# Retention stage of a float32 encoder block: three v groups moved to its front, its steps spaced two pieces apart, PSUM in two alternating pools

## The chip, the cores and the metric

The kernel runs on one core of one Trainium2 chip. The core has five engines with queues of their own: TensorE (PE: matmuls), VectorE (DVE), ScalarE (ACT), GpSimd (POOL) and SyncE (SP, here only for loads). The metric is the device time of one execution in microseconds; a version's time is the median of several executions.

## The reference

One layer of an encoder on x of 512 tokens by 2048 channels, float32:

```python
h = rmsnorm(x, norm_gain)
q, k, v, g_ret, c_b, c_c, c_x, g_conv, merge_logits = split(h @ w_in)   # 8 of 1024 columns, then 2 x 2048
o = bidirectional_retention(rotary(q), rotary(k) * 128**-0.5, v)        # 8 heads of 128, decay per head and direction
branch_ret = rmsnorm_per_head(o) * ret_gn_gain * silu(g_ret)
branch_conv = c_b * conv3(c_c * c_x) * silu(g_conv)                     # depthwise, along the tokens
merged = sum over n of sigmoid(merge_logits[n]) * (branches[n] @ w_branch[n])   # w_branch: 2 of 1024 x 2048
out = rmsnorm(x + merged @ w_out, final_gain)
```

## The kernel before, in words

**Arithmetic.** Each float32 product is made of three products of rounded parts (`mm3`, L165 to L167): high by high, high by low, low by high. Tensors that are multiplied exist as a high part, made by ACT (`split_to`, L160), and a low part, the rest, made by DVE (L161).

**Pieces.** All weights pass through one list, `pieces`: 512 KB each (4 tiles of 128 rows by 256 columns). SP loads a piece to `raw` (L125), ACT makes `whi`, DVE makes `wlo`, PE uses it. `run` works the list off: it loads up to three pieces ahead, splits two ahead, issues a piece's matmuls, and then the functions of one entry of the list `background`. A scheduler then orders the instructions of each engine by their readiness, so the engine's order isn't exactly that of the text.

**Stages.** (1) Stage A, to some 150 us: x is normalised to `h1`, `h00`, `h10` (parts of h transposed, in SBUF), and 4 k groups (`group`) and 2 v groups (`group_tok`) of w_in's columns are computed, 4 pieces each. The k groups go through `rotary_post`, the v groups through `v_post` (ACT, L481, four evictions from PSUM, scaled), to DRAM (`k_d`, `v_d`). In the background `token_forms` adds the token sums that the next stage wants (L293 to L301, then a split to `fm`), one for each of eight j. (2) The Strassen stage, to 954 us: 40 groups (`group_s`) for the remaining columns of w_in, 7 products instead of 8, 4 pieces each, 42 matmuls of 256 columns a piece, with sums of weights on DVE (L154 to L156) and `combine` (L280 to L287) on ACT and DVE after each group. The results are scaled and stored by POOL's queue (`gate_d`, `conv_d`, `g_d`, `q_d`). (3) The retention stage, to 1164 us: the groups of `w_branch[1]` (conv branch, `up_group(1, i)`, 2 pieces each of 24 matmuls of 512 columns) in turn with v groups 2 and 3 (4 pieces each of 48 matmuls of 256 columns), and in the background `retention_program`, the 8 heads. (4) The groups of `w_branch[0]` (retention branch), to 1251 us. (5) `w_out` and the final norm.

**One head** is made of: `fetch_head` (k and q from DRAM to `st`), `split_head` (to `kh`, `kl`, `qh`, `ql`), `decay_table` (`tb`), four `score` (three matmuls to `sp`, DVE multiplies with the table at L514, then a split to `sh`, `sl`), four `outp` (three matmuls `op <- sh, vh`), `square`, `rms_o` (two matmuls with `ones`, L542 and L543), and `finish`. 26 matmuls of 512 columns each head. DMA issues of POOL (`nc.gpsimd.dma_start`) go through one queue in order: loads of k, q, v, gates, the conv operand and stores of results.

**Order before the change.** `retention_program` deals 27 steps to 21 places in order:

```python
        n = 21
        return [[]] + [sum(steps[k * len(steps) // n : (k + 1) * len(steps) // n], []) for k in range(n)]
```

PSUM: a Strassen group takes two tiles of two banks each from a pool `p4` of four, in turn. That pool is closed and a pool of two, `psR`, and the retention's pool `rps` are opened at the retention stage.

Of the kernel before, what the change touches and what calls it, by code (L numbers as in the profile page):

```python
# [30 lines left out]
def hybrid_block_kernel(  # L31
# [43 lines left out]
    gate_d = dr.tile([2, KT, P, S], F32, name="gate_d")  # L75
    ret_d = dr.tile([GG, P, S], F32, name="ret_d")
    conv_d = dr.tile([GG, P, S], F32, name="conv_d")
# [91 lines left out]
    background = []  # L169
    later = []  # L170

# [5 lines left out]
    def run(upto):  # L177
        while state["used"] < upto:
            i = state["used"]
            while state["loaded"] < min(i + 4, state["limit"]):  # L180
                load(pieces[state["loaded"]])
                state["loaded"] += 1
            split_upto(i + (3 if i >= XC - 1 else 1))
            pieces[i]["use"](pieces[i])
            state["used"] += 1
            for x in later:
                x[0] -= 1
            while later and later[0][0] < 0:
                later.pop(0)[1]()
            if background:  # L190
                for f in background.pop(0):
                    f()
# [33 lines left out]
    def group_s(src, post):  # L226


        st = {}

        order = [
            (0, 0, "b11", "d4"), (0, 1, "b12", "a11"), (1, 1, "b22", "a12"), (1, 0, "u", "a22"),
            (3, 0, "z", "a7"), (3, 1, "w", "d6"), (2, 0, "v", "a1"),
        ]
        seen = [next(i for i, o in enumerate(order) if o[0] == b) for b in range(4)]
        for q in range(KT // 4):
            def use(pc, q=q):
                if q == 0:
                    tiles = [fin["p4"].tile([P, 2, S], F32, name="acc", tag="acc") for _ in range(2)]
                    st["acc"] = tiles if state["banks"] else tiles[::-1]  # L240
                    state["banks"] += 1
                for n, (bank, half, b, a) in enumerate(order):
                    acc = st["acc"][bank // 2][:, bank % 2, half * 256 : half * 256 + 256]
                    for r in range(2):
                        x = token_form(a, q + 4 * r)
                        mm3(
                            acc,
                            [weight_form(w, b, r) for w in pc["w"]],
                            (x[:, 0], x[:, 1]),
                            q == 0 and r == 0 and n in seen,  # L250
                            q == KT // 4 - 1 and r == 1,
                            skip_group_check=True,
                        )
# [252 lines left out]
    def score(h, m):  # L506
# [7 lines left out]
        nc.vector.scalar_tensor_tensor(s, sp, SCALE, hd["tb"][:, o0 : o0 + S], op0=ALU.mult, op1=ALU.mult)  # L514
        sh = rps["sb"].tile([P, S], F32R, name="sh", bufs=3)
        sl = rps["sb"].tile([P, S], F32R, name="sl", bufs=3)
        split_to(sh, sl, s)
# [9 lines left out]
    def square(h):  # L527
        hd = heads[h]
        sq = tmp()
        nc.scalar.activation(sq, hd["o"], AF.Square)  # L530
        sh = rps["sb"].tile([P, S], F32R, name="sh", bufs=3)
        sl = rps["sb"].tile([P, S], F32R, name="sl", bufs=3)
        nc.vector.tensor_copy(sh, sq)
        nc.vector.tensor_tensor(sl, sq, sh.bitcast(F32), op=ALU.subtract)
        hd["sq"] = (sh, sl)
# [15 lines left out]
    def finish(h):  # L551
# [7 lines left out]
        nc.vector.tensor_tensor(y, y, hd["g"], op=ALU.mult)  # L559
        if h < 4:  # L560
            nc.gpsimd.dma_start(out=ret_d[h], in_=y)
# [24 lines left out]
    def split_head(h):  # L586
        hd = heads[h]
        for n in ("k", "q"):
            hi = rps["sb"].tile([P, S], F32R, name=n + "h")
            lo = rps["sb"].tile([P, S], F32R, name=n + "l")  # L590
            split_to(hi, lo, hd[n + "f"])
            hd[n] = (hi, lo)
# [5 lines left out]
    def open_branch():  # L598
        br0 = rps["br0"] = big.tile([P, 2, GG, S], F32R, name="br0", tag="h1")
        brs[0] = lambda kt: [(0, br0[:, :, kt, :])]  # L600
        for i in range(2):
            load_branch(0, i)

    def retention_program():

        L = lambda f, *v: (lambda: f(*v))
        steps = [[] for _ in range(6 * (H // 2) + 3)]
        for i in range(H // 2):
            a, b = 2 * i, 2 * i + 1
            own = [  # L610
                [L(split_v, i), L(split_head, a), L(decay_table, a), L(fetch_head, b)],
                [L(score, a, 0), L(score, a, 1)],
                [L(outp, a, 0), L(outp, a, 1), L(score, a, 2), L(score, a, 3), L(fetch_g, a)],
                [L(outp, a, 2), L(outp, a, 3), L(square, a), L(split_head, b), L(decay_table, b)],
                [L(score, b, 0), L(score, b, 1), L(rms_o, a)] + ([L(fetch, i + 1), L(fetch_head, a + 2)] if b + 1 < H else []),
                [L(outp, b, 0), L(outp, b, 1), L(score, b, 2), L(score, b, 3), L(finish, a), L(fetch_g, b)],
                [L(outp, b, 2), L(outp, b, 3), L(square, b)],
                [L(rms_o, b)],
                [L(finish, b)],
            ]  # L620
            for k, s in enumerate(own):
                steps[6 * i + k] += s
        steps[16].insert(0, open_branch)
        n = 21
        return [[]] + [sum(steps[k * len(steps) // n : (k + 1) * len(steps) // n], []) for k in range(n)]

# [5 lines left out]
    for i in range(4):  # L632
# [4 lines left out]
        else:  # L637
            group(cols(BW, i), KT, hTf, kp)
    for i in range(2):
        group_tok(cols(2 * BW, i), v_post(i))  # L640
    n_a = len(pieces)
# [107 lines left out]

    for n in range(2):  # L750
        up_group(1, n, conv_up_post(n))
    for i in range(2, 4):
        group_tok(cols(2 * BW, i), v_post(i))
        up_group(1, i, conv_up_post(i))
    for i in range(4, 8):
        up_group(1, i, conv_up_post(i))
# [4 lines left out]

    def load_branch(n, i):
        d = (ret_d, conv_d)[n]
        t = T()
        nc.gpsimd.dma_start(out=t, in_=pair(d, i))
        k = slice(2 * i, 2 * i + 2)
# [103 lines left out]
    state["loaded"] = 1  # L870
    ps_x = tc.tile_pool(name="xps", bufs=4, space=PSUM)
    xps = ps_x.__enter__()
# [29 lines left out]
    log_decays()  # L902
    ps_x.__exit__(None, None, None)
    xst.close()
    for z in range(2):
# [8 lines left out]
    part["forms"] = fm[::-1]  # L914
    for j in range(KT // 2):
        background.extend([[lambda j=j: token_forms(j)], []])
    run(n_a)
    while background:
        for f in background.pop(0):
            f()  # L920
    psx.close()
    h10x.close()
    with tc.tile_pool(name="p4", bufs=4, space=PSUM) as p4:
        fin["p4"] = p4
        lr = ctx.enter_context(tc.tile_pool(name="lr", bufs=1, reuse_waits="tile"))
        fin["lr"] = lr
        fin["sd"] = lr.tile([P, 2 * WF], F32, name="sd", tag="ev")
        run(n_s)
    fms.close()
    hx.close()  # L930

    pools["ps"] = ctx.enter_context(tc.tile_pool(name="psR", bufs=2, space=PSUM))
    pools["wp"] = ctx.enter_context(tc.tile_pool(name="wpR", bufs=3, reuse_waits="tile"))
# [7 lines left out]
    for _ in range(3):  # L941
        load(pieces[state["loaded"]])
        state["loaded"] += 1
    for i in range(4):
        load_branch(1, i)
    split_upto(n_s + 2)
    while later:
        later.pop(0)[1]()
    rsx.close()
    ha = lr.tile([P, 2, 7, 256], F32R, name="h10", tag="ev")  # L950
    hb = lr.tile([P, WF], F32R, name="h10b", tag="raw4")
    hb = hb[:, :512].rearrange("p (z j s) -> p z j s", z=2, j=1)
    hold["h10"] = lambda j: hb[:, :, 0] if j == 7 else ha[:, :, j]
    for z in range(2):
        nc.gpsimd.dma_start(out=ha[:, z], in_=a21_d[z, 0:7].rearrange("j p s -> p j s"))
        nc.gpsimd.dma_start(out=hb[:, z], in_=a21_d[z, 7:8].rearrange("j p s -> p j s"))
    ret = ExitStack()
    rps["sb"] = ret.enter_context(tc.tile_pool(name="ret", bufs=2, side="right", reuse_waits="tile"))
    rps["p"] = ret.enter_context(tc.tile_pool(name="rps", bufs=2, space=PSUM))
    dist = rps["dist"] = rps["sb"].tile([P, TW], F32, name="dist", bufs=1)  # L960
# [4 lines left out]
    nc.gpsimd.iota(dist, pattern=[[1, TW]], base=-OFF, channel_multiplier=-1, allow_small_or_imprecise_dtypes=True)  # L965
    fetch(0)
    fetch_head(0)
    background.extend(retention_program())
    run(n_r - 2)
    while background:  # L970
        for f in background.pop(0):
            f()
    rps["stg"] = big.tile([P, 2, 2, 2, S], F32, name="stg", tag="h00")
    for i in range(2):
        load_merge(i)
    run(n_r)
    ret.close()
    bbx.close()
# [61 lines left out]
```

## Time and profile before

| what | us |
|---|---|
| median of 3 runs | 1435.68 |
| lowest and highest | 1434.04, 1437.82 |
| the profiled execution | 1437.88 |
| its span in the profile | 1436.1 |
| PE busy | 1401.9 |
| DVE busy | 1083.8 |
| ACT busy | 586.8 |
| POOL busy | 104.7 |

The profile is of one execution of its own; its span runs from the first to the last recorded instruction. "Busy" of PE is the time covered by its matmuls' records, which are pipelined: one starts before the record of the one before it has ended. PEclk, in windows, is the clock granted to PE as a share of its full 2.4 GHz. L12 is line 12 of the kernel before.

### The profile page before, as it was taken

How to read it: one execution, taken by the hardware profiler on the slowest of the kernel's cores; microseconds unless marked ns; L12 is line 12 of the kernel's file. 1: busy time of each engine (PE TensorE's matmuls, PEld its weight loads, DVE VectorE, ACT ScalarE, POOL GpSimd, SP SyncE). 2: the span in 40 equal slices, each digit the busy share in tenths (PEclk: the TensorE clock that was granted, in tenths of full speed). 3: DMA queues.
4: the chain of work that ended last, by engine and by line, in shares of the span. 5: the costliest groups of instructions: out<-in, count | busy, mean ns of one | idle time of the engine just before them, and what ended most of it. 6: DMA issues, size and time to landing. Idle time of an engine off the chain costs nothing.

```text
span 1436.1 us, 23571 instructions
## 1 busy us (share of the span) xinstructions
PE 1401.9 (98%) x9938; PEld 1315.1 (92%) x9938; DVE 1083.8 (75%) x1417; ACT 586.8 (41%) x590; POOL 104.7 (7%) x141
## 2 busy tenths in 40 slices
PE   8999999999999999999999999988998999999997
PEld 7899999999999999999999999977896788888886
DVE  4877789999899888898898998956786845523533
ACT  7343344444434334343343443444565532222421
POOL 0000000000000000000000000021113101111110
PEclk9999999999999999999999999999999999999999
DMA  7533433344334344333343333476437445553412
GB/s 246 166 118 120 131 118 118 118 122 143 118 118 133 106 142 135 118 118 118 122 141 120 118 118 119 135 231 213 138 128 241 146 148 191 186 215 98 155 66 102
DMA packets 151310, 202.36 MB, mean 141 GB/s; under 512 B 6900, under 2 KB 127780, under 8 KB 150564
## 3 DMA queue, kind: packets, MB, share of 16 engines
q1 hardware_dynamic: 132788, 143.17, 31.7%
q0 software_dynamic: 18384, 57.68, 11.7%
q8 instruction: 77, 1.26, 0.4%
q14 instruction: 29, 0.24, 0.1%
q10 hardware_dynamic: 32, 0.01, 0.0%
HBM read 170.43 MB, written 30.41 MB: 140 GB/s over the span
## 4 chain that ended last, share of the span: by engine, by line
PE 88%; DMA 4%; DVE 3%; issue 2%; ACT 1%; SPq 0%; POOL 0%; DVEq 0%; POOLq 0%; ACTq 0%
PE acc L165 29%; PE acc L167 29%; PE acc L166 29%; DMA raw<-in_w_in_dram 1%; DVE wlo L161 1%; DMA st<-k_d 1%; DMA v_d<-T 0%; DMA T<-conv_d 0%; DMA xb<-in_x_dram 0%; PE op L165 0%; DMA stg<-m_d 0%; PE op L166 0%; PE op L167 0%; PE xtp L384 0%; SPq L373 0%
## 5 line engine op out<-in xcount | busy, mean ns | idle before, releaser
L160 ACT ACTIVATE whi<-raw 128x1792 fp32r<-128x1792 f32 (+2 forms) x257 | 374.8, 1459 | 579.2 <-PE acc L166 425.5
L161 DVE TENSOR_TENSOR wlo<-raw,whi 128x1792 fp32r<-128x1792 f32 (+2 forms) x257 | 442.7, 1724 | 209.0 <-PE acc L167 83.6
L165 PE MATMUL acc<-fm,whi 128*128 128x256 f32 x1280 | 362.6, 283 | 1.7 <-ACT T L481 1.7
L167 PE MATMUL acc<-fm,wlo 128*128 128x256 f32 x1280 | 363.1, 284 | 0.4 <-DVE wlo L161 0.4
L166 PE MATMUL acc<-fm,whi 128*128 128x256 f32 x1280 | 362.1, 283 | 0.0
L165 PE MATMUL acc<-h,whi 128*128 128x256 f32 (+1 forms) x1152 | 330.0, 286 | 0.0
L167 PE MATMUL acc<-h,wlo 128*128 128x256 f32 (+1 forms) x1152 | 328.4, 285 | 0.0
L166 PE MATMUL acc<-h,whi 128*128 128x256 f32 (+1 forms) x1152 | 328.3, 285 | 0.0
L165 PEld LDWEIGHTS acc<-fm,whi 128*128 128x128 f32 x1280 | 245.2, 192 | 1.9 <-ACT T L481 1.9
L167 PEld LDWEIGHTS acc<-fm,wlo 128*128 128x128 f32 x1280 | 244.4, 191 | 0.6 <-DVE wlo L161 0.6
L166 PEld LDWEIGHTS acc<-fm,whi 128*128 128x128 f32 x1280 | 244.4, 191 | 0.0
L165 PEld LDWEIGHTS acc<-h,whi 128*128 128x128 f32 x1152 | 216.9, 188 | 2.5
L166 PEld LDWEIGHTS acc<-h,whi 128*128 128x128 f32 x1152 | 216.5, 188 | 2.6
L167 PEld LDWEIGHTS acc<-h,wlo 128*128 128x128 f32 x1152 | 216.4, 188 | 2.5
L154 DVE TENSOR_TENSOR raw<-raw 128x512 f32<-128x512 f32 x160 | 109.7, 686 | 18.7 <-DMA raw<-in_w_in_dram 18.4
L166 PE MATMUL acc<-wlo,mT 128*128 128x512 f32 (+1 forms) x272 | 103.5, 380 | 0.0
L165 PE MATMUL acc<-whi,mT 128*128 128x512 f32 (+1 forms) x272 | 103.0, 379 | 0.0
L167 PE MATMUL acc<-whi,mT 128*128 128x512 f32 (+1 forms) x272 | 102.1, 375 | 0.0
L167 PE MATMUL acc<-whi,h 128*128 128x256 f32 x252 | 71.0, 282 | 0.0
L166 PE MATMUL acc<-wlo,h 128*128 128x256 f32 x252 | 71.0, 282 | 0.0
L165 PE MATMUL acc<-whi,h 128*128 128x256 f32 x252 | 71.0, 282 | 0.0
L156 DVE TENSOR_TENSOR raw<-raw 128x256 f32<-128x256 f32 x160 | 67.8, 424 | 3.8
(205 smaller groups left out, 1763.6 us busy)
## 6 DMA issues: line engine op xcount, KB each, us to landing
raw<-in_w_in_dram SPq DMA_DIRECT2D x191, 512.0 KB, 3.8
raw<-in_w_branch_dram SPq DMA_DIRECT2D x32, 512.0 KB, 3.8
raw<-in_w_out_dram SPq DMA_DIRECT2D x32, 512.0 KB, 3.7
gate_d<-T POOLq DMA_DIRECT2D x16, 512.0 KB, 4.7
T<-gate_d POOLq DMA_DIRECT2D x8, 512.0 KB, 5.3
m_d<-T POOLq DMA_DIRECT2D x8, 512.0 KB, 3.7
stg<-gate_d POOLq DMA_DIRECT2D x8, 512.0 KB, 4.5
stg<-m_d POOLq DMA_DIRECT2D x8, 512.0 KB, 4.0
```

What stands on the lines that cost most here:

```text
L154: nc.vector.tensor_tensor(s[:, 0:2].rearrange("p f r x -> p r f x"), diag, both21, op=ALU.add)
L156: nc.vector.tensor_tensor(s[:, 2], b21, b12, op=ALU.add)
L160: pin(nc.scalar.activation(hi, src, AF.Copy))
L161: pin(nc.vector.tensor_tensor(lo, src, hi.bitcast(F32), op=ALU.subtract))
L165: pin(nc.tensor.matmul(acc, lh, rh, start=start, stop=False, **kw))
L166: pin(nc.tensor.matmul(acc, lh, rl, start=False, stop=False, **kw))
L167: pin(nc.tensor.matmul(acc, ll, rh, start=False, stop=stop, **kw))
```

## The change

- **Order of the pieces.** Stage A computes one v group, not two. The retention stage begins with three v groups (12 pieces), and the eight conv groups (16 pieces) follow.
- **Spacing of the steps.** `retention_program` has 29 steps, three per head, the first of which runs ahead of the stage's pieces, and the others one behind each of 28 pieces. A head's `score` stand in its steps 1 and 2, its `outp` in 3 and 4, `rms_o` in 6, `finish` in 7. `sh` and `sl` have 5 buffers instead of 3, the splits of k and q one instead of two. Within a step the functions are sorted by a rank.
- **Branch operands.** The four loads of the conv branch stand behind the pieces of the v groups, in places 0, 2, 4 and 6, their splits a place later; before, they stood ahead of the stage. Of the retention branch only heads 0 and 1 go through DRAM, not 0 to 3.
- **The queue at the stage's start.** Loads of head 0's k and q and of v are written ahead of the reload of `h10`.
- **PSUM.** `xps`, the pool of stage A's transposes, stands on the right side; behind it `px`, two tiles of two banks. Strassen groups take both tiles from `px` and from `psA` in turn. The retention stage's groups use `px`.
- **Token forms** are made in the order 0, 4, 1, 5, 2, 6, 3, 7.

```diff
-                    tiles = [fin["p4"].tile([P, 2, S], F32, name="acc", tag="acc") for _ in range(2)]
-                    st["acc"] = tiles if state["banks"] else tiles[::-1]
+                    pool = (fin["px"], pools["ps"])[state["banks"] % 2]
+                    st["acc"] = [pool.tile([P, 2, S], F32, name="acc", tag="acc") for _ in range(2)]
...
-        sh = rps["sb"].tile([P, S], F32R, name="sh", bufs=3)
-        sl = rps["sb"].tile([P, S], F32R, name="sl", bufs=3)
+        sh = rps["sb"].tile([P, S], F32R, name="sh", bufs=5)
+        sl = rps["sb"].tile([P, S], F32R, name="sl", bufs=5)
...
-        if h < 4:
+        if h < 2:
             nc.gpsimd.dma_start(out=ret_d[h], in_=y)
...
     def retention_program():
...
+        first = (outp, score, rms_o, square, fetch_branch, fetch, fetch_head, fetch_g, split_head, decay_table)
...
+        steps = [[] for _ in range(3 * H + 5)]
+        for h in range(H):
+            i = h // 2
             own = [
...
+                [L(split_head, h), L(decay_table, h)] + ([L(fetch_head, h + 1)] if h + 1 < H else []),
+                [L(score, h, 0), L(score, h, 1)],
+                [L(score, h, 2), L(score, h, 3), L(fetch_g, h)],
+                [L(outp, h, 0), L(outp, h, 1)],
+                [L(outp, h, 2), L(outp, h, 3), L(square, h)],
+                [],
+                [L(rms_o, h)],
+                [L(finish, h)],
             ]
+            if h % 2 == 0:
+                own[1].insert(0, L(split_v, i))
+            elif h + 1 < H:
+                own[1].append(L(fetch, i + 1))
             for k, s in enumerate(own):
-                steps[6 * i + k] += s
...
+                steps[3 * h + k] += s
...
-    for i in range(2):
-        group_tok(cols(2 * BW, i), v_post(i))
+    group_tok(cols(2 * BW, 0), v_post(0))
...
-    for n in range(2):
-        up_group(1, n, conv_up_post(n))
-    for i in range(2, 4):
+    for i in range(1, 4):
         group_tok(cols(2 * BW, i), v_post(i))
-        up_group(1, i, conv_up_post(i))
-    for i in range(4, 8):
+    for i in range(8):
         up_group(1, i, conv_up_post(i))
...
-    for j in range(KT // 2):
+    for j in (0, 4, 1, 5, 2, 6, 3, 7):
...
-    for i in range(4):
-        load_branch(1, i)
     split_upto(n_s + 2)
...
+    fetch_head(0)
+    fetch(0)
...
+    steps = retention_program()
+    for f in steps.pop(0):
+        f()
+    for i in range(4):
+        steps[2 * i].append(lambda i=i: fetch_branch(1, i))
+        steps[2 * i + 1].append(lambda i=i: split_branch(1, i))
+    background.extend(steps)
```

**How the instructions move.** POOL's queue at the start of the retention stage, before (`h10` and `h10b` are the two parts of the reload of `h10` from `a21_d`, `T<-conv_d` the loads of the conv operand, `st` those of k and q):

```order
L956 DMA h10b_10355<-a21_d_83 128x256 x2
L652 DMA gate_d_75<-T_10100 128x2x512
L765 DMA T_10329<-conv_d_77 128x2x512
L765 DMA T_10333<-conv_d_77 128x2x512
L955 DMA h10_10354<-a21_d_83 128x7x256
L652 DMA gate_d_75<-T_10295 128x2x512
...
L955 DMA h10_10354<-a21_d_83 128x7x256
...
L568 DMA T_10372<-v_d_82 128x1024
L584 DMA st_10374<-k_d_79 128x512
L584 DMA st_10376<-q_d_80 128x512
```

Two loads of the conv operand stand ahead of the reload's second part, v, k and q behind it. POOL's queue at the same place in the changed kernel:

```order
L953 DMA h10b_10124<-a21_d_83 128x256 x2
L650 DMA gate_d_75<-T_9876 128x2x512
L563 DMA T_10121<-v_d_82 128x1024
L759 DMA T_10230<-conv_d_77 128x2x512
L952 DMA h10_10123<-a21_d_83 128x7x256
L650 DMA gate_d_75<-T_10071 128x2x512
L579 DMA st_10117<-k_d_79 128x512
L579 DMA st_10119<-q_d_80 128x512
L952 DMA h10_10123<-a21_d_83 128x7x256
```

One load of the conv operand is left there, v has moved ahead of the reload, k and q stand between the reload's two parts.

PE in the retention stage before, from the first `sp` of a head in the middle of the stage to its first `op` (`b0` and `b1` are tiles of the conv operand, the matmuls into `acc` those of a conv piece):

```order
L165 MATMUL sp_10934<-qh_10854,kh_10850 128x512
L166 MATMUL sp_10934<-ql_10855,kh_10850 128x512
L167 MATMUL sp_10934<-qh_10854,kl_10851 128x512
L165 MATMUL acc_10996<-b0_10319,whi_10782 128x512
L166 MATMUL acc_10996<-b0_10319,whi_10782 128x512
...
L165 MATMUL sp_10944<-qh_10854,kh_10850 128x512
...
L165 MATMUL sp_10968<-qh_10854,kh_10850 128x512
...
L165 MATMUL sp_10978<-qh_10854,kh_10850 128x512
L165 MATMUL op_10961<-sh_10940,vh_10846 128x512
```

Matmuls of a conv piece stand singly between the scores, and the first `op` comes right behind the last `sp`'s first matmul. In the changed kernel the same for a head beside two v pieces (matmuls into `acc` from `h00`, `h1`):

```order
L165 MATMUL sp_10711<-qh_10641,kh_10637 128x512
L166 MATMUL sp_10711<-ql_10642,kh_10637 128x512
L167 MATMUL sp_10711<-qh_10641,kl_10638 128x512
L165 MATMUL sp_10721<-qh_10641,kh_10637 128x512
...
L165 MATMUL acc_10491<-whi_10566,h00_93 128x256
L166 MATMUL acc_10491<-wlo_10567,h00_93 128x256
...
L165 MATMUL sp_10810<-qh_10641,kh_10637 128x512
...
L165 MATMUL acc_10840<-whi_10653,h1_92 128x256
L166 MATMUL acc_10840<-wlo_10654,h1_92 128x256
...
L167 MATMUL acc_10840<-whi_10653,h1_92 128x256
L165 MATMUL op_10889<-sh_10717,vh_10744 128x512
L166 MATMUL op_10889<-sl_10718,vh_10744 128x512
```

Before, the first `op` stood among the scores of its own head; now two times 48 matmuls of v pieces lie between a score and the `op` that reads it.

DVE where stage A goes over into the Strassen stage, before (L293 to L301 the additions of a token form, L154 to L156 the weight sums of a Strassen piece, `fm` and `wlo` low parts):

```order
L301 TENSOR_TENSOR T_1432<-T_1428,T_1432 128x256
L154 TENSOR_TENSOR raw_1493<-raw_1493 128x2x2x128
L161 TENSOR_TENSOR fm_622<-T_1432,fm_622 128x1024
L161 TENSOR_TENSOR wlo_1441<-raw_1368,whi_1440 128x1024
L155 TENSOR_TENSOR raw_1493<-raw_1493 128x2x128
L156 TENSOR_TENSOR raw_1493<-raw_1493 128x256
L154 TENSOR_TENSOR raw_1547<-raw_1547 128x2x2x128
L161 TENSOR_TENSOR wlo_1496<-raw_1438,whi_1495 128x1024
...
L161 TENSOR_TENSOR wlo_1550<-raw_1493,whi_1549 128x1792
...
L161 TENSOR_TENSOR wlo_1607<-raw_1547,whi_1606 128x1792
```

The token form's split is through ahead of the first low part of a Strassen piece that stands here. In the changed kernel, where these lines have the numbers L288 to L296:

```order
L154 TENSOR_TENSOR raw_1317<-raw_1317 128x2x2x128
L154 TENSOR_TENSOR raw_1374<-raw_1374 128x2x2x128
...
L161 TENSOR_TENSOR wlo_1320<-raw_1253,whi_1319 128x1792
L161 TENSOR_TENSOR fm_625<-T_1311,fm_625 128x1024
...
L154 TENSOR_TENSOR raw_1452<-raw_1452 128x2x2x128
L161 TENSOR_TENSOR wlo_1377<-raw_1317,whi_1376 128x1792
L288 TENSOR_TENSOR T_1437<-h00_93 128x256
L288 TENSOR_TENSOR T_1437<-h10_113 128x256
L288 TENSOR_TENSOR T_1437<-h1_92 128x512
...
L294 TENSOR_TENSOR T_1441<-T_1437 128x512
...
L295 TENSOR_TENSOR T_1441<-T_1437,T_1441 128x256
L161 TENSOR_TENSOR wlo_1455<-raw_1374,whi_1454 128x1792
```

Before, the last token form was through ahead of the first Strassen piece's low part; now the last one's additions stand between the low parts of the second and the third piece.

## Rows read from the trace of the kernel before

**Rows 1.** The page, part 1: busy us (share of the span) xinstructions of each engine.

```profile
PE 1401.9 (98%) x9938; PEld 1315.1 (92%) x9938; DVE 1083.8 (75%) x1417; ACT 586.8 (41%) x590; POOL 104.7 (7%) x141
```

**Rows 2.** PE's waits: what waited and for what: us in total, times, longest us.

```profile
PE op L165 <- ACT sh L160: 9.9, 6, 2.6
...
PE acc L165 <- ACT T L481: 1.7, 1, 1.7
PE acc L165 <- DVE T L287: 1.6, 1, 1.6
```

**Rows 3.** Windows of the retention stage: from:to, us, each engine's busy us, PEclk, DMA share.

```profile
954.00:967.00 13.00, 7.56 (x31) 5.20 (x30) 6.80 (x8) 3.60 (x4) 6.91 (x10) 1.00 0.86 253
...
1030.40:1034.50 4.10, 4.10 (x11) 3.22 (x12) 4.10 (x8) 2.48 (x5) 0.53 (x1) 0.58 0.40 128
...
1088.00:1094.00 6.00, 4.12 (x13) 2.68 (x13) 2.50 (x4) 1.57 (x2) 3.25 (x5) 0.88 0.90 294
1094.00:1100.00 6.00, 4.78 (x13) 3.30 (x12) 3.02 (x4) 3.49 (x4) 1.43 (x2) 0.55 0.85 305
...
sum 210.00, PE 190.76 PEld 159.55 DVE 152.59 ACT 109.71 POOL 39.65; mean PE 8.67 PEld 7.25 DVE 6.94 ACT 4.99 POOL 1.80
```

**Rows 4.** Windows about the Strassen stage's start and inside it, same columns.

```profile
125.00:165.00 40.00, 37.96 (x319) 37.56 (x319) 23.46 (x32) 14.61 (x16) 1.11 (x2) 1.00 0.38 121
...
200.00:400.00 200.00, 200.00 (x1680) 200.00 (x1680) 188.56 (x231) 86.69 (x63) 5.02 (x7) 1.00 0.39 124
```

**Rows 5.** PE's timeline at three places: start us, us, what [idle before <-releaser].

```profile
954.03 0.28 PE L167 MATMUL acc<-fm,wlo 128*128 128x256 f32 x1
955.90 0.70 PE L165 MATMUL acc<-b,whi 128*128 128x512 f32 x2 [1.59 <-DVE T L287]
...
998.03 0.28 PE L165 MATMUL acc<-whi,h 128*128 128x256 f32 x1
998.15 0.28 PE L166 MATMUL acc<-wlo,h 128*128 128x256 f32 x1
...
1163.57 0.39 PE L167 MATMUL acc<-b,wlo 128*128 128x512 f32 x1
1163.80 0.39 PE L165 MATMUL acc<-br,whi 128*128 128x512 f32 x1
```

**Rows 6.** POOL's timeline at the retention stage's start, same columns.

```profile
959.17 0.72 POOL L765 DMA_DIRECT2D T<-conv_d  x1
...
963.96 0.55 POOL L584 DMA_DIRECT2D st<-k_d  x1
964.50 0.54 POOL L584 DMA_DIRECT2D st<-q_d  x1
```

**Rows 7.** DMA issues near 958.4 and 964: queue, count, KB, us to landing.

```profile
gate_d<-T POOLq DMA_DIRECT2D x1, 512.0 KB, 4.7
...
st<-k_d POOLq DMA_DIRECT2D x1, 256.0 KB, 7.5
st<-q_d POOLq DMA_DIRECT2D x1, 256.0 KB, 8.0
```

**Rows 8.** The critical chain, in its part of the first retention head: start us, us.

```profile
993.99 0.62 ACT sh L160
994.64 1.29 DVE sl L161 x2
```

**Rows 9.** DVE's timeline, last token form and first pieces of the Strassen stage.

```profile
129.29 1.35 DVE L293 TENSOR_TENSOR T<-h 128x256 f32<-128x256 f32 x3
130.68 0.69 DVE L299 TENSOR_TENSOR T<-T 128x512 f32<-128x512 f32 x1
...
131.41 0.43 DVE L300 TENSOR_TENSOR T<-T 128x256 f32<-128x256 f32 x1
...
134.05 1.22 DVE L161 TENSOR_TENSOR fm<-T,fm 128x1024 fp32r<-128x1024 f32 x1
...
154.35 2.02 DVE L161 TENSOR_TENSOR wlo<-raw,whi 128x1792 fp32r<-128x1792 f32 x1
```

More of the change, by code (lines that the diff above doesn't have):

```diff
@@ L75, in hybrid_block_kernel @@
     gate_d = dr.tile([2, KT, P, S], F32, name="gate_d")
-    ret_d = dr.tile([GG, P, S], F32, name="ret_d")
+    ret_d = dr.tile([2, P, S], F32, name="ret_d")
     conv_d = dr.tile([GG, P, S], F32, name="conv_d")
@@ L169, in hybrid_block_kernel @@
     background = []
-    later = []
     def split_upto(n):
@@ L185, in run @@
             state["used"] += 1
[L186 to L189, printed above, removed]
             if background:
@@ L530, in square @@
         nc.scalar.activation(sq, hd["o"], AF.Square)
-        sh = rps["sb"].tile([P, S], F32R, name="sh", bufs=3)
-        sl = rps["sb"].tile([P, S], F32R, name="sl", bufs=3)
+        sh = rps["sb"].tile([P, S], F32R, name="sh", bufs=5)
+        sl = rps["sb"].tile([P, S], F32R, name="sl", bufs=5)
         nc.vector.tensor_copy(sh, sq)
@@ L588, in split_head @@
         for n in ("k", "q"):
-            hi = rps["sb"].tile([P, S], F32R, name=n + "h")
-            lo = rps["sb"].tile([P, S], F32R, name=n + "l")
+            hi = rps["sb"].tile([P, S], F32R, name=n + "h", bufs=1)
+            lo = rps["sb"].tile([P, S], F32R, name=n + "l", bufs=1)
             split_to(hi, lo, hd[n + "f"])
@@ L600, in open_branch @@
         brs[0] = lambda kt: [(0, br0[:, :, kt, :])]
-        for i in range(2):
-            load_branch(0, i)
     def retention_program():
[L606 to L609, printed above, removed]
-            own = [
[L611 to L619, printed above, removed]
-            ]
+        first = (outp, score, rms_o, square, fetch_branch, fetch, fetch_head, fetch_g, split_head, decay_table)
@@ new lines, in retention_program @@
+        rank = lambda f: first.index(f) if f in first else len(first)
+        L = lambda f, *v: (rank(f), lambda: f(*v))
+        steps = [[] for _ in range(3 * H + 5)]
+        for h in range(H):
+            i = h // 2
+            own = [
+                [L(split_head, h), L(decay_table, h)] + ([L(fetch_head, h + 1)] if h + 1 < H else []),
[6 more added lines that the diff above has]
+                [L(finish, h)],
+            ]
+            if h % 2 == 0:
+                own[1].insert(0, L(split_v, i))
+            elif h + 1 < H:
+                own[1].append(L(fetch, i + 1))
@@ L621, in retention_program @@
             for k, s in enumerate(own):
-                steps[6 * i + k] += s
-        steps[16].insert(0, open_branch)
-        n = 21
-        return [[]] + [sum(steps[k * len(steps) // n : (k + 1) * len(steps) // n], []) for k in range(n)]
+                steps[3 * h + k] += s
+        steps[12].append(L(fetch_branch, 0, 0))
+        steps[13].append((-1, open_branch))
+        steps[14].append(L(split_branch, 0, 0))
+        return [[f for _, f in sorted(s, key=lambda x: x[0])] for s in steps]
@@ L638, in hybrid_block_kernel @@
             group(cols(BW, i), KT, hTf, kp)
-    for i in range(2):
-        group_tok(cols(2 * BW, i), v_post(i))
+    group_tok(cols(2 * BW, 0), v_post(0))
     n_a = len(pieces)
@@ L760, in hybrid_block_kernel, with fetch_branch, split_branch @@
     n_up = len(pieces)
[L762 to L765, printed above, removed]
+    def fetch_branch(n, i):
+        t = brs[n, i] = T()
+        nc.gpsimd.dma_start(out=t, in_=pair((ret_d, conv_d)[n], i))
+    def split_branch(n, i):
+        t = brs[n, i]
         k = slice(2 * i, 2 * i + 2)
@@ L870, in hybrid_block_kernel @@
     state["loaded"] = 1
-    ps_x = tc.tile_pool(name="xps", bufs=4, space=PSUM)
+    ps_x = tc.tile_pool(name="xps", bufs=4, space=PSUM, side="right")
     xps = ps_x.__enter__()
@@ L903, in hybrid_block_kernel @@
     ps_x.__exit__(None, None, None)
+    fin["px"] = ctx.enter_context(tc.tile_pool(name="px", bufs=2, space=PSUM, side="right"))
     xst.close()
@@ L920, in hybrid_block_kernel @@
             f()
-    psx.close()
[L922 to L928, printed above, removed]
+    h10x.close()
+    lr = ctx.enter_context(tc.tile_pool(name="lr", bufs=1, reuse_waits="tile"))
+    fin["lr"] = lr
+    fin["sd"] = lr.tile([P, 2 * WF], F32, name="sd", tag="ev")
+    run(n_s)
+    psx.close()
     fms.close()
     hx.close()
-    pools["ps"] = ctx.enter_context(tc.tile_pool(name="psR", bufs=2, space=PSUM))
+    pools["ps"] = fin["px"]
     pools["wp"] = ctx.enter_context(tc.tile_pool(name="wpR", bufs=3, reuse_waits="tile"))
@@ L943, in hybrid_block_kernel @@
         state["loaded"] += 1
-    for i in range(4):
-        load_branch(1, i)
     split_upto(n_s + 2)
-    while later:
-        later.pop(0)[1]()
     rsx.close()
+    ret = ExitStack()
+    rps["sb"] = ret.enter_context(tc.tile_pool(name="ret", bufs=2, side="right", reuse_waits="tile"))
+    rps["p"] = ret.enter_context(tc.tile_pool(name="rps", bufs=2, space=PSUM))
+    fetch_head(0)
+    fetch(0)
     ha = lr.tile([P, 2, 7, 256], F32R, name="h10", tag="ev")
@@ L956, in hybrid_block_kernel @@
         nc.gpsimd.dma_start(out=hb[:, z], in_=a21_d[z, 7:8].rearrange("j p s -> p j s"))
-    ret = ExitStack()
-    rps["sb"] = ret.enter_context(tc.tile_pool(name="ret", bufs=2, side="right", reuse_waits="tile"))
-    rps["p"] = ret.enter_context(tc.tile_pool(name="rps", bufs=2, space=PSUM))
     dist = rps["dist"] = rps["sb"].tile([P, TW], F32, name="dist", bufs=1)
@@ L965, in hybrid_block_kernel @@
     nc.gpsimd.iota(dist, pattern=[[1, TW]], base=-OFF, channel_multiplier=-1, allow_small_or_imprecise_dtypes=True)
-    fetch(0)
-    fetch_head(0)
-    background.extend(retention_program())
+    steps = retention_program()
[5 more added lines that the diff above has]
+    background.extend(steps)
     run(n_r - 2)
-    while background:
-        for f in background.pop(0):
-            f()
     rps["stg"] = big.tile([P, 2, 2, 2, S], F32, name="stg", tag="h00")
@@ L976, in hybrid_block_kernel @@
     run(n_r)
+    while background:
+        for f in background.pop(0):
+            f()
     ret.close()
```

## The prediction, made before the changed kernel ran

> **What bounds the kernel now.** I read the page's first part first: TensorE (PE) is busy 98% of the span [rows 1]. So only what PE loses counts, and the views to read next are PE's waits, then the windows in which it is not full. The waits name few causes [rows 2]: `op`, the retention's second product, waits for ScalarE's split `sh` (9.9 us in 6 waits), the first v post's eviction (`T L481`) is waited for once (1.7), the last Strassen group's combine (`T L287`) once (1.6). The windows place them. In the Strassen stage PE is busy all 200.00 us of 200:400 and its granted clock is 1.00 [rows 4]; there is nothing to gain there, and nothing else than the waits named at its two ends. In the retention stage, 954 to 1164, PE is busy 190.76 of 210.00 us [rows 3], which leaves 19.24 idle, 5.44 of it in the first 13 us. There the clock also falls after idle stretches: 0.58 in 1030.4:1034.5, 0.88 in 1088:1094, 0.55 in 1094:1100 [rows 3] (0.5 is the 1.2 GHz level, 1.00 the 2.4 GHz one).
>
> **What the retention stage loses.** Three terms. Idle: 19.24. Slow clock, by the busy time of its three windows: 4.10 x 0.42 + 4.12 x 0.12 + 4.78 x 0.45 = 4.4. Restart: a 256-column matmul follows the one before it after 0.12 us [rows 5], but its record lasts 0.28, so a wait costs 0.16 more than the idle time printed for it (954.03 to 955.90 is 1.87, less 0.12, for 1.59 idle); for the 13 waits that PE's timeline has in this stage 2.1. Together 25.7 us.
>
> **The stage's start.** Now PE needs the conv branch's operand `b` before its first matmul (4 loads of `conv_d`, then splits on ACT and DVE) and waits for the PSUM that the last combine reads: 955.90 instead of 954.15 [rows 5], and more up to 967. The changed kernel begins with a v group, whose operands (`h00`, `h1`) stand in SBUF and whose accumulator comes from the pool that the last group did not use. This start costs nothing: the weights of the first three pieces are loaded ahead as before. Behind it the conv loads have 12 pieces, 12 x 48 x 0.119 = 68 us, to arrive and be split (0.119 is 200.00 us over 1680 matmuls [rows 4]). The cover is ample, if it were gone the 5.44 us would be back.
>
> What is late next is the first head. By the order, 86 v matmuls stand ahead of the first `sp`: 954.15 + 86 x 0.119 = 964.4. It needs head 0's k and q. Their loads now stand on POOL's queue behind one `h10` reload and the last `gate_d` store, in the place where the first `T<-conv_d` issue stood at 959.17 [rows 6], so they issue at 959.2 and 959.7 instead of 963.96 and 0.55 later. How long do they take? Bounds from rows: 4.7 as the `gate_d` store issued just before [rows 7], 7.5 and 8.0 as k and q themselves took, issued when two `h10` reloads, four conv loads and v were in the air [rows 7]. In the new place one reload, the store and the weights are in the air; I take 5.0 and 5.6, near the lower row. q lands at 965.3, ScalarE's split (0.62 [rows 8]) makes 965.9, DVE's low half another 0.645 (two in 1.29 [rows 8]) 966.6, and PE reaches that one a matmul later: 1.6 + 0.4 = 2.0 us lost. Bounds: nothing (q by 963.8), and 4.5 (8.0 us for q). The second `h10` reload, one issue later, is wanted only by the third v piece's second half, 954.15 + 2 x 5.71 + 2.9 = 968.5 without and some 973 with the scores between; issued at 960.3 it has 8 to 12 us, against 8 for the slowest load here. No term.
>
> By the Trainium skill, "DMA: Bandwidth & Descriptors", section "Issuing engines are not separate DMA queues", transfers of all issuing engines interleave on the same 16 DMA engines, so an earlier place on POOL's queue does not keep k and q clear of SP's weight loads. The rows agree in part: a 256 KB load took 7.5 while a 512 KB store 5 us earlier took 4.7 [rows 7]. By it q would take its 8.0 again, the loss would be 4.5 instead of 2.0, and the sum 1414.1.
>
> **The rest of the stage.** The old program has 27 steps for 21 places, so neighbours fall together and a head's `op` follows its `sp` within a piece or so. Between them run DVE's scaling (some 0.6), ScalarE's 0.62 and DVE's 0.645 [rows 8], 1.9 us of work behind whatever else the two queues hold in order; `op` came up to 2.6 us late [rows 2]. The new program has one step per place, 28 places, and two pieces between: a conv piece is 24 matmuls at 0.23 us [rows 5], 5.5, and a third of a head's 26 matmuls another 2.0, so two pieces are some 15 us of cover in place of some 4. `sh` and `sl` get 5 buffers so that four stand at once. DVE has the same work as before plus four low halves of the moved v group, 152.59 [rows 3] + 4 x 1.22 [rows 9] = 157.5 us, in a stage of some 210 us: 75%, that is 5.6 of 7.5 us a place. It would have to fall 10 us behind for a wait as before. So I let the waits go, and with them the slow stretches, each of which follows a wait, and put 1.0 for small ones (0 to 3). k's and q's split buffers fall from 2 to 1: a head's split is then bound to the scores of the head before, which end a place earlier (7.5 us of cover).
>
> **The Strassen stage's start.** The v group taken out of stage A, 4 x 5.71 = 22.9 us, is run in the retention stage: no change of PE work. Of 125:165 PE loses 2.04 idle [rows 4], 1.7 of it the v eviction that held the pool of PSUM (ACT T L481), plus 0.3 of restarts: 2.3. The Strassen groups now start in the other pool, so the eviction is off the path. But stage A is 22.9 shorter for the same eight token forms on DVE. The order has the last form's additions between the low halves of pieces 1 and 2. A form is 1.35 + 0.69 + 2 x 0.43 + 1.22 = 4.1 us of DVE [rows 9], a piece's sums and low half 0.69 + 2 x 0.43 + 2.02 = 3.6, against 42 x 0.119 = 5.0 of PE a piece. Walking DVE's list from the stage's end near 128 with these durations, the low halves of pieces 1 to 3 come 0.2, 0.4 and 0.3 us after PE asks: 0.9. Bounds: nothing, and 4.1 (the whole form on the path). Gain 2.3 - 0.9 = 1.4.
>
> **Alternating pools.** Before, a group took the next two of four tiles in a ring; group n+2 got group n's tiles back. Now it takes both tiles of one pool of two, then both of the other: group n+2 again gets group n's. No instruction is added, and in 200:400 no wait exists [rows 4]: 0.
>
> **Sum.** 25.7 less 2.0 and 1.0 is 22.7, and 1.4: 24.1 us. The profiled execution took 1437.88, 1.8 over its span and 2.2 over the median: 1437.88 - 24.1 = 1413.8, in the median's terms **1411.6**. With every loss at nothing 1407.7; with every one at its upper end (4.5, 3, 4.1) 1419.3. So the likeliest case has 1408 to 1419.
>
> **Rivals.**
> - *Half the gain comes back.* Each queue runs in order. A `wlo` behind a head's scaling and splits, or a score behind a `tb` table, makes new waits, and the clock falls after them. For: stretches like 1088:1100 lost 1.88 + 1.22 idle and 2.6 of clock [rows 3], and DVE's average hides dense places. Against: 15 us of cover. Two stretches of 6 us: 1424.
> - *The change does not do what it says*: the waits of `op` are not of distance but of DVE's and ScalarE's total load, and move along. Then only the two starts gain, 3.4 + 1.4 us, and the fourth v group in this stage (4 low halves, 4.9 us of DVE) takes that back: about 1435.
> - *Slower: the pools make every Strassen group wait.* If the allocator holds a pool until both tiles of the group two before it are released at once, each of the 39 boundaries waits for the combine, 1.59 us as at 955.90 [rows 5]: 62 us, 1474. It decides from 24.1 / 39 = 0.62 us a boundary. For: the last combine was waited for, before the retention stage. Against: that pool was closed and handed on whole, and by the order group n+1's first tile is free since the group before last, a whole group (20 us) earlier.
>
> The Trainium skill, "TensorE: Matmul & The Clock Gate", section "A second HAM failure mode: psum-queue depth-cycling", speaks for that rival in another form: it tells of a kernel that cycled through PSUM banks at each iteration, idled shortly between groups and had its clock swing between the two levels. Nothing in 200:400 shows it [rows 4], where four banks are cycled too; at 1.7 to 2.6 us a fall [rows 3] it would cost 39 times that, and the time would be some 1475 to 1510.
>
> **How the numbers follow.** Likeliest 0.71, half back 0.14, 0.05 for a gain that something unnamed eats down to a few us over the bound below, no effect 0.05, pools 0.05. A measurement of this kernel tells 0.3%, some 4 us, from no change: faster 0.90, same 0.05, slower 0.05. Range: from a little under the best sum, 1406, to the half-back rival, 1424.
>
> **What would show it.** Right: no idle at the step from the Strassen to the retention stage; `op <- sh` gone from PE's waits; granted clock 1.00 all through the retention stage; one wait of `sp` near 964 to 968, for q; in 125:150 small waits for `wlo` in place of that for `T L481`; DVE near 157 us in the retention stage. Wrong: waits at group boundaries in 200:800, or clock under 1.00 with conv pieces running.

## The result, and the profile after

The changed kernel takes 1413.74 us (median of 4 runs, 1411.70 to 1417.45), beside 1436.75 for the kernel before (4 runs, 1434.04 to 1440.95): ratio 0.984, 95% interval 0.9807 to 0.9873. The prediction was 1411.6, range 1406 to 1424. Two repeats gave 1412.17 against 1439.62 (0.9809, 0.979 to 0.9828) and 1411.48 against 1440.66 (0.980, 0.9777 to 0.9823).

The page's first part, for the row of [rows 1]:

```profile
span 1413.8 us, 23552 instructions
...
PE 1397.6 (99%) x9938; PEld 1317.2 (93%) x9938; DVE 1083.0 (77%) x1418; ACT 587.3 (42%) x591; POOL 102.7 (7%) x138
```

PE's waits after, all that are left once x is in; they answer to [rows 2]:

```profile
PE sp L165 <- ACT qh L160: 2.9, 1, 2.9
```

The evictions `T L481`, the combine `T L287` and all of `op <- sh` are gone. So is the longest single wait before, which the prediction didn't name: the norm's first matmul waited 3.1 us for DVE (L514).

What had held `op <- sh` before is read from ACT, which makes `sh`. These are a wait of PE and one of ACT, and a stretch of the critical chain (start us, us):

```profile
PE sp L542 <- DVE tmp L514: 3.1, 1, 3.1
...
ACT br L160 <- DMA T<-ret_d: 6.1, 2, 3.8
```

```profile
1025.94 1.28 ACT L547
1027.23 0.63 ACT tmp L547
1027.92 1.25 issue
1029.17 0.63 ACT tmp L548
1029.80 0.53 ACT sh L160
1030.38 0.50 PE op L165
```

L547 and L548 are two functions of the norm in `rms_o`. Each loads a table first, in 1.28 us here; the chain shows the second load as `issue`. Together they take 3.8 us of ACT ahead of `sh`, and `op` at 1030.38 waits 2.61. The same stands ahead of the wait at 1120 (1.90), and its second function ahead of that at 1103 (0.46). Ahead of those at 1091 (1.88) and 1096 (1.22) ACT stands still for a load from `ret_d`, which the split `br` needs (2.32 and 3.76 us), and ahead of that at 995 (1.83) for q (2.56 us). So each of the six waits was for a `sh` that stood behind something longer in ACT's queue. The change touches this in three ways: there are two places between a score and its `op`; one `ret_d` load is left, and its split stands two places behind it; and no place holds both scores and a norm.

The one wait that is left is the first score's, for q, as forecast. Windows of the changed kernel's retention stage, which now runs from 932 to 1142, for [rows 3]:

```profile
942.00:946.00 4.00, 1.10 (x8) 0.90 (x8) 0.99 (x2) 1.26 (x2) 0.57 (x1) 0.95 1.17 296
946.00:960.00 14.00, 14.00 (x88) 12.70 (x89) 9.91 (x15) 8.44 (x11) 1.81 (x3) 0.89 0.47 155
...
1040.00:1060.00 20.00, 20.00 (x89) 16.47 (x88) 19.80 (x27) 11.84 (x16) 5.09 (x8) 1.00 0.71 237
...
sum 210.00, PE 207.10 PEld 182.11 DVE 155.55 ACT 116.39 POOL 38.34; mean PE 17.26 PEld 15.18 DVE 12.96 ACT 9.70 POOL 3.19
```

The stage is as long as before, 210 us, with a v group (22.9 us of PE) more in it. Idle is 2.90 in place of 19.24; the clock is below 1.00 only at and behind that wait (0.95 and 0.89), where it costs 14.00 x 0.11 = 1.5 us. DVE has 155.55 busy (157.5 forecast). In 1040:1060 DVE is busy 19.80 of 20.00 and PE has no idle; e8, with half the distance, is full there too (112.00 of 1030:1142). The Strassen stage's start, and the stage itself, for [rows 4]:

```profile
100.00:145.00 45.00, 45.00 (x384) 45.00 (x383) 36.34 (x52) 17.41 (x17) 1.28 (x2) 1.00 0.41 130
200.00:400.00 200.00, 200.00 (x1680) 200.00 (x1680) 187.35 (x231) 86.84 (x63) 5.01 (x7) 1.00 0.39 124
```

No idle time at all, at the start as at the groups' boundaries.

The wait that is left, in the chain of work that ended last (start us, us):

```profile
934.49 1.00 POOL h L952
...
937.38 0.57 POOL st L579
937.95 7.06 DMA st<-q_d
945.01 0.02 issue
945.04 0.64 ACT qh L160
...
945.72 1.22 PE sp L165 x2
```

POOL issued k and q behind the `h10` reload, as the order said; q's transfer took 7.06 us.

### The profile page after: what moved, and what is told of

Same layout as the page of the kernel before. It is cut to its first block, busy times and chain, and to the rows that moved or that the text cites. A ratio compares the mean times of both kernels' runs of the same rounds, so it can differ in the third digit from the quotient of the medians.

```text
span 1413.8 us, 23552 instructions
## 1 busy us (share of the span) xinstructions
PE 1397.6 (99%) x9938; PEld 1317.2 (93%) x9938; DVE 1083.0 (77%) x1418; ACT 587.3 (42%) x591; POOL 102.7 (7%) x138
## 4 chain that ended last, share of the span: by engine, by line
PE 97%; DMA 1%; SPq 0%; DVE 0%; issue 0%; POOL 0%; ACT 0%; DVEq 0%; POOLq 0%; ACTq 0%
PE acc L165 31%; PE acc L167 31%; PE acc L166 31%; PE sp L165 1%; PE sp L166 1%; PE sp L167 1%; PE op L166 1%; PE op L167 1%; PE op L165 1%; DMA st<-q_d 0%; DMA xb<-in_x_dram 0%; PE xtp L379 0%; SPq L368 0%; PE sp L537 0%; PE sp L538 0%
## 5 line engine op out<-in xcount | busy, mean ns | idle before, releaser
L154 DVE TENSOR_TENSOR raw<-raw 128x512 f32<-128x512 f32 x160 | 109.4, 685 | 8.2 <-DMA raw<-in_w_in_dram 8.2
L156 DVE TENSOR_TENSOR raw<-raw 128x256 f32<-128x256 f32 x160 | 67.7, 423 | 3.7
```

The source lines that it names most:

```text
L154: nc.vector.tensor_tensor(s[:, 0:2].rearrange("p f r x -> p r f x"), diag, both21, op=ALU.add)
L156: nc.vector.tensor_tensor(s[:, 2], b21, b12, op=ALU.add)
```

## The experiments

All but e1 are edits of the changed kernel. Each is set against the kernel before on the same chip: a0, e2, e3 and e4 share one such measurement (1439.62), e1, e5, e6 and e7 one (1439.29), a1 and e8 one (1440.66).

**a0, a1: the changed kernel again.** 

> The changed kernel again, as the measure for the runs beside it: 1413.7 us, PE's only wait in the retention stage the one of the first score for q, 2.9 us, with the clock under 1.00 behind it.

> The changed kernel once more, beside the next run: 1412 to 1414 us.

Measured 1412.17 (5 runs, 1411.71 to 1412.86) and 1411.48 (4 runs, 1410.28 to 1414.48). PE's wait for q is 1.7 and 2.0 us here, in the first profile 2.9.

**e1: the pools alone, in the kernel before.**

```diff
-                    tiles = [fin["p4"].tile([P, 2, S], F32, name="acc", tag="acc") for _ in range(2)]
+                    pool = (fin["px"], pools["ps"])[state["banks"] % 2]
+                    st["acc"] = [pool.tile([P, 2, S], F32, name="acc", tag="acc") for _ in range(2)]
```

> The kernel before with the alternating PSUM pools alone (pieces, steps and loads as before). Theory: at the Strassen stage's start the v eviction no longer holds PE (1.8 us less); at the retention stage's start the conv operand's low half is only split at 958.2, so the 1.6 us that the combine held turn into a wait for the operand: 1434 to 1435 us. Rival: both waits go, 3.6 us less, 1432.5. Rival (the pools cost): waits at the Strassen groups' boundaries, 1440 and more.

Measured 1436.81 (10 runs, 1435.74 to 1441.40) against 1439.29, ratio 0.9986 (0.9974 to 0.9997): 2.0 to 2.5 us, with an interval of 0.4 to 3.7. The time is outside the forecast 1434 to 1435; the theory's mechanism is what the waits show:

```profile
PE op L165 <- ACT sh L160: 9.0, 6, 2.6
PE acc L166 <- DVE b L161: 3.4, 1, 3.4
...
PE acc L167 <- DVE wlo L161: 1.6, 2, 1.1
```

Both PSUM waits are gone, and where the combine was waited for the operand `b` is now: 3.4 us in one wait. Of 125:165 PE loses 0.47 us (before 2.04 [rows 4]), waiting for `wlo`; the other 1.1 us for `wlo` are in the retention stage:

```profile
125.00:165.00 40.00, 39.53 (x335) 39.33 (x334) 24.44 (x33) 14.61 (x16) 1.11 (x2) 1.00 0.41 133
945.00:970.00 25.00, 20.48 (x110) 17.44 (x109) 13.18 (x15) 9.39 (x10) 8.70 (x13) 0.86 0.92 288
```

So the gain at the Strassen stage's start comes from the pools. At the retention stage's start they uncover the next waits: in 945:970 PE loses 4.52 us, against 5.44 before [rows 3], and the clock is at 0.86 there, where it was 1.00. The gain there needs the v groups in front.

**e3: the new order of pieces, pools and loads, with the old steps.**

```diff
+        n = 21
+        steps = [[]] + [sum(steps[k * len(steps) // n : (k + 1) * len(steps) // n], []) for k in range(n)]
```

> The changed kernel with the order of its pieces, its pools and its loads, but the steps of before: 27 dealt to 21 places, so that neighbours fall together. Theory (the clumps make the waits): the start of the stage gains as in the changed kernel, the waits of op come back in the four clumps, 8 to 14 us of idle time and 3 to 5 of slow clock: 1424 to 1432 us. Rival (the order of the pieces alone): v groups first take the conv operand and the PSUM off the path, and that is nearly all: 1413 to 1417.

The edit also takes out the sorting within a place, and takes back what the change did to the retention branch: four heads go through DRAM again, with two loads, each split one place behind its load.

Measured 1426.60 (4 runs, 1425.20 to 1428.91), ratio 0.9909 (0.9888 to 0.993): 13 us of the gain are there, 14 are not. PE's waits, ACT's timeline ahead of the longest of them, one of ACT's waits, and two windows:

```profile
PE op L165 <- ACT sh L160: 9.3, 4, 3.8
PE acc L167 <- DMA h<-a_d: 1.4, 1, 1.4
```

```profile
1060.48 1.06 ACT L160 ACTIVATE br<-T 128x1024 fp32r<-128x1024 f32 x1 [4.83 <-DMA T<-ret_d]
1061.56 1.28 ACT L542 ACT_TABLE_LOAD   x1
...
1064.02 1.28 ACT L543 ACT_TABLE_LOAD   x1
...
1065.85 0.61 ACT L160 ACTIVATE sh<-tmp 128x512 fp32r<-128x512 f32 x1
```

```profile
ACT br L160 <- DMA T<-ret_d: 7.6, 2, 4.8
```

```profile
1060.00:1072.00 12.00, 8.20 (x24) 5.89 (x24) 7.33 (x11) 9.46 (x12) 1.27 (x2) 0.72 0.18 61
...
1083.00:1095.00 12.00, 9.35 (x29) 7.11 (x28) 9.68 (x14) 7.44 (x12) 1.73 (x3) 0.72 0.51 184
```

`op <- sh` is back with 9.3 us in four waits. One (2.61 us, at 998) stands in a place with two steps. The longest (3.80, at 1067) and a short one (0.29, at 1037) stand in the place behind such a one, and the last (2.65, at 1086) in a place with one step. What all four have in common is a norm on ACT just ahead of `sh`. Ahead of the two at 1067 and 1086 ACT also stands still for a `ret_d` load, 4.83 and 2.77 us, before the norm; it is at these two that the clock falls to 0.72, which costs 8.20 x 0.28 + 9.35 x 0.28 = 4.9 us. So the time is the theory's, and the order alone is half of the gain, but that the clumps make the waits is not shown. The other half is a bundle of dealing, distance, sorting, the norm's place and the retention branch's loads, and no run takes them apart. The second row of PE's waits is a wait of its own: with no scores ahead of the third v piece, the second part of the `h10` reload is late.

**e2: `op` one piece behind its scores, `finish` where it was.**

```diff
-                [L(score, h, 2), L(score, h, 3), L(fetch_g, h)],
-                [L(outp, h, 0), L(outp, h, 1)],
+                [L(outp, h, 0), L(outp, h, 1), L(score, h, 2), L(score, h, 3), L(fetch_g, h)],
                 [L(outp, h, 2), L(outp, h, 3), L(square, h)],
                 [],
+                [],
```

> The changed kernel with a head's op products one piece behind its scores, not two, the steps as evenly dealt as before. Theory (cover): one piece of 48 matmuls at 0.119 or 24 at 0.227 is 5.5 us and more, the scaling and splits of two scores take 2.5 us of DVE and 1.2 of ACT; so only where something else stands in the queues are there waits: 1414 to 1419 us, op waits under 3 us in total. Rival (distance itself): two pieces are needed; each of eight heads waits 1 to 2.6 us as before, clock falls behind them: 1424 to 1432.

Measured 1417.74 (4 runs, 1415.93 to 1419.67), 5.6 us above a0 and within the theory's range. Its one new wait:

```profile
PE op L165 <- DVE tmp L553: 2.2, 1, 2.2
```

L553 is the product in `finish` that reads an older head's `op` from PSUM. The wait is for that bank; for `sh` no `op` waits in e2, at any of the eight heads. So e2 prices the distance together with `finish`. e8 moves `finish`, and the norm with it:

**e8: as e2, with the norm and `finish` a piece earlier too** (the added empty step left out again).

> The changed kernel with op one piece behind its scores, and the norm and the finish a piece earlier as well, so that a head's PSUM is free two pieces before the next but one wants it, as in the changed kernel. In the run with finish left where it was, the one wait of op was released by the finish of an earlier head (DVE L553), which holds the PSUM of op. Theory (one piece is cover enough for the splits): no wait of op, the time of the changed kernel within 2 us. Rival (distance itself): op still waits, for sh or sl, 2 us or more with the clock down behind it, 3 to 6 us slower than the changed kernel.

Measured 1414.93 (4 runs, 1412.81 to 1415.26) beside 1411.48: 3.4 us slower by the medians, but the ratios to before, 0.9814 (0.9796 to 0.9832) and 0.980 (0.9777 to 0.9823), overlap. Its new wait, and the timelines of DVE and of ACT ahead of it:

```profile
PE op L165 <- ACT sh L160: 1.6, 1, 1.6
```

```profile
986.63 0.43 DVE L528 CAST sh<-tmp 128x512 fp32r<-128x512 f32 x1 [4.08 <-ACT tmp L525]
986.98 0.68 DVE L550 SCALAR_TENSOR_TENSOR tmp<-tmp 128x512 f32<-128x512 f32 x1
...
988.78 1.22 DVE L161 TENSOR_TENSOR vl<-T,vh 128x1024 fp32r<-128x1024 f32 x1
...
991.25 1.22 DVE L161 TENSOR_TENSOR wlo<-raw,whi 128x1024 fp32r<-128x1024 f32 x1
992.38 0.68 DVE L554 TENSOR_TENSOR tmp<-tmp,g 128x512 f32<-128x512 f32 x1
992.98 1.28 DVE L509 SCALAR_TENSOR_TENSOR tmp<-sp,tb 128x512 f32<-128x512 f32 x2
```

```profile
982.40 1.28 ACT L543 ACT_TABLE_LOAD   x1
...
984.24 1.04 ACT L160 ACTIVATE whi<-raw 128x1024 fp32r<-128x1024 f32 x1
985.18 0.94 ACT L498 ACTIVATE tb<-tb 128x896 f32<-128x896 f32 x1
986.02 0.58 ACT L525 ACTIVATE tmp<-op 128x512 f32<-128x512 f32 x1
```

The scores were written by 987. DVE is busy without a gap from 986.63 and comes to scale them at 992.98, behind an older head's `finish`, the v split and a weight's low half: 6 us of queue, which one v piece (48 x 0.119 = 5.7) does not cover and two do. Ahead of it DVE had stood still for 4.08 us, waiting for the square on ACT (L525), which came behind a norm, a weight's high half and a decay table. How much of the 6 us gathered in that time isn't shown. That happens at one head of eight. So neither expectation is met whole: there is one wait of `op`, of 1.6 us, and a loss that isn't clear of the noise.

**e4: k and q of head 0 loaded ahead, to a T tile free earlier.**

```diff
+        if h == 0:
+            t = T()
+            for j, (n, d) in enumerate((("k", k_d), ("q", q_d))):
+                hd[n + "f"] = t[:, j]
+                nc.gpsimd.dma_start(out=t[:, j], in_=d[h])
+            return
...
-        steps[2 * i].append(lambda i=i: fetch_branch(1, i))
-        steps[2 * i + 1].append(lambda i=i: split_branch(1, i))
+        steps[2 * i + 1].append(lambda i=i: fetch_branch(1, i))
+        steps[2 * i + 2].append(lambda i=i: split_branch(1, i))
```

> The changed kernel with k and q of head 0 loaded to a T tile that is free some 11 us earlier, ahead of the last Strassen group's end, and the conv operand's loads a place later. Theory: the wait of 2.9 us for q's transfer and the slow clock behind it (some 1.9) go: 1408.5 to 1410 us, PE without a wait in the whole stage. Rival (the wait moves): the splits now queue behind the last group's scaling on ACT and DVE, or the v operand or the decay table becomes the last: a wait of 1 us or more stays, 1412 to 1414.

Measured 1409.45 (4 runs, 1408.95 to 1410.01) beside a0's 1412.17, whose lowest run is 1411.71. The best version of this study. Windows and waits:

```profile
120.00:140.00 20.00, 19.79 (x167) 19.58 (x166) 16.14 (x26) 9.99 (x10) 0.56 (x1) 1.00 0.40 134
930.00:1135.00 205.00, 205.00 (x1175) 180.81 (x1174) 155.27 (x210) 115.71 (x152) 38.10 (x59) 1.00 0.58 189
```

```profile
PE acc L167 <- DVE wlo L161: 0.5, 2, 0.3
```

PE is full through the whole retention stage, at full clock. The time is the theory's, 1408.5 to 1410. The gain is 2.7, not the 4 to 5 that it was reckoned from: a0's wait is 1.7 where the first profile's was 2.9, and at the Strassen stage's start two small waits for `wlo` show.

**e5: token forms in the order 0 to 7.** (`for j in range(KT // 2)`)

> The changed kernel with the token forms in the order 0 to 7. Theory: the first Strassen piece wants forms 0 and 4, and both are long done; only the last form matters, 7 in both orders, wanted by the fourth piece there and here: no wait of over 0.5 us between 125 and 165, time as the changed kernel's 1411 to 1418. Rival: DVE's order changes enough that a low half or a form is late at the stage's start: a wait of 1 to 4 us there.

One run, 1414.04; a wait of 0.3 for `wlo` at the Strassen stage's start, nothing else new. In this one run the order of the forms is worth nothing that shows.

**e6: all Strassen groups in one pool of two tiles.** (`pool = fin["px"]`)

> The changed kernel with all Strassen groups in the one pool of two tiles, so that each group takes the tiles of the group just before it. Theory (tiles come free one by one): the first tile's last reader (DVE L279, 931.62 + 0.68) is done before the last matmul of the group (932.39), and the second is wanted 24 matmuls, 2.9 us, later, when the combine is over; waits of 0 to 0.3 us at the 39 boundaries, 1413 to 1427 us. Rival (the pool comes free as a whole): each boundary waits 1.6 us and restarts, 68 us, 1482, and more where the clock falls.

One run, 1443.70, some 30 us slower; both expectations miss. The wait, and DVE's timeline at the longest:

```profile
PE acc L165 <- DVE sd L279: 20.4, 11, 3.3
```

```profile
214.67 0.68 DVE L278 TENSOR_TENSOR T<-sd,acc 128x512 f32<-128x512 f32 x1
215.26 2.02 DVE L161 TENSOR_TENSOR wlo<-raw,whi 128x1792 fp32r<-128x1792 f32 x1
217.20 0.68 DVE L279 TENSOR_TENSOR sd<-sd,acc 128x512 f32<-128x512 f32 x1
```

Tiles do come free one by one, and PE waits at only 11 of 39 boundaries; there the combine's second step (L279) stands behind a low half on DVE, which is nearly full. The waits make 20.4 of the 30 us; the rest isn't worked out. With two pools, or before with a ring of four tiles, no such wait is seen.

**e7: 3 buffers of `sh` and `sl`.** (`bufs=3`)

> The changed kernel with 3 buffers of sh and sl, as before, not 5; PE's order is the same. Theory: the fourth score's split cannot be written before the first op has read its own, a place later, and ACT and DVE stand still meanwhile with the weight splits behind them; weights are split two pieces ahead, so part of it is covered: PE waits of 0.5 to 2 us in most heads, 1418 to 1432 us. Rival: the lead of the weights covers all of it: 1412 to 1417, no new wait of PE.

One run, 1414.23; no new wait of PE. My theory fell: PE shows no loss with three buffers. The rival has the time; that it is the weights' lead which covers isn't shown.

## Why the prediction came out right, point by point

- **Sum and sizes.** The gain was put at 24.1 us; the medians differ by 23.0, in the repeats by 27.4 (1439.62 - 1412.17) and 29.2 (1440.66 - 1411.48), the two profiled spans by 22.3. 24.1 lies between the first and the repeats. The first 44 us, which the change does not aim at, differ from profile to profile: PE is busy 39.66 us there in the first profile of the changed kernel, with the clock at 0.83 in 10:20, and 41.28 in a0's, whose span is 1410.1.
- **The stage's start.** Right: no wait at the step into the retention stage, and q last, behind 86 v matmuls. Loads were estimated at 5.0 and 5.6; k took 5.0 in the first profile and q 7.06, so the wait was 2.9, not 2.0 with its restart. In the repeats q took 5.89 (a0) and 6.12 (a1), and the waits were 1.7 and 2.0, which is the estimate. The prediction took 8.0 for q as what follows where transfers interleave, by the Trainium skill, "DMA: Bandwidth & Descriptors", section "Issuing engines are not separate DMA queues". No profile here has 8.0, though all three loads are above the 4.7 of the lower row. What the sum left out at this wait is the clock behind it, 1.5 us more in the first profile. It was priced for the old waits and forgotten for the new one, and the sign "granted clock 1.00 all through the retention stage" was not met there.
- **The second part of the `h10` reload** was called safe at 8 us. It landed 10.6 us after its issue at 938.49; the scores and the wait ahead of it hid that, and e3, which has none there, waits 1.4 us. "No term" was right by its cover, not by its size.
- **The rest of the stage.** Right in the result: the waits of `op` and the slow clock are gone, and in e3 they come back (14.4 us against a0). Why is shown in part. The prediction counted 1.9 us of work between score and `op` and left the rest at "whatever else the two queues hold"; the traces name it: norms of 3.8 us and splits that wait for their loads, both on ACT. That the distance took them off the path, and not the norm's place or the later split of the one load that is left, isn't separated by e3. That two places are needed is not shown: with one, e2 loses 5.6 us at a PSUM bank and e8 some 3, not clear of the noise.
- **The Strassen stage's start.** 0.9 us of loss was forecast; the first profile and both repeats show none, e4 and e5 0.5 and 0.3. The eviction went off the path as forecast, and e1 shows that it was the pools that did it.
- **The pools.** 0, as forecast. The slower rival's price per boundary was wrong in kind: even one pool of two waits only where DVE is late (e6). The sum beside it, 39 falls of 1.7 to 2.6 us, comes to 1478 to 1513 rather than 1475 to 1510.
- **Half the gain back** did not happen; its mechanism, a queue on DVE of 6 us, is seen once in e8.

In all, from 1439.6: the order of the pieces, the pools and the loads at the stage's start give 13.0 (e3). The even dealing at one piece's distance, with the sorting, the norm's place and the fewer loads of the retention branch, gives another 9 (by e2) to 11 (by e8), not taken apart; the second place 5.6 (e2) or 3.4 (e8, not clear of the noise); the early load of k and q (e4) another 2.7.

## What to carry to other kernels

When a list of small steps runs beside a stream of large pieces, look at what stands ahead of the awaited instruction in the helper engine's queue. Here it was a norm of 3.8 us, or a split that waited for its own load. So it is worth trying to keep such work out of the places where a product is split for the next matmul, and to put a split some places behind its load; neither was tried by itself here. Measure the distance against the longest such stretch (6 us of DVE in e8), not against the mean load. A stage should begin with the pieces whose operands already stand on the chip, and what its first helper step reads should be loaded into whatever buffer is free earliest (2.7 us in e4).

## What was not expected of the hardware

Two idle stretches of the same length in e6, 3.22 us at 424 and at 631, were followed by a granted clock of 0.88 and of 1.00; PE had been full ahead of both. In e3 a wait of 2.61 us at 998 was followed by 1.00, one of 2.65 at 1086 by 0.72. So the clock after a wait is not settled by the wait's length alone in these rows:

```profile
428.00:442.00 14.00, 14.00 (x108) 14.00 (x107) 10.40 (x13) 4.47 (x3) 0.71 (x1) 0.88 0.34 113
...
635.00:649.00 14.00, 14.00 (x120) 14.00 (x119) 9.94 (x13) 4.47 (x3) 0.72 (x1) 1.00 0.40 128
```

A term of slow clock per wait, as the prediction had it for the old waits, is a mean.
